# An encoder layer's mixing stage: dilated heads third, latent heads last

## Chip, cores and metric

The kernel runs on one core of a Trainium2 chip. The metric is device time of one execution in microseconds (us), as the median of several. About 0.3% (6.3 us) is what a measurement of this kernel can tell from no change.

## What is computed

A trunk of two layers over 512 tokens of width 1024, in 32-bit floats. Each layer has a gated feed-forward block, a mixing stage with four groups of four heads, a second feed-forward block and a gated per-layer input. Cut to the mixing stage:

```python
z = rms_norm(x, mix_norm[i]) @ w_in[i]
z_na, z_swa, z_dil, z_mla = jnp.split(z, IN_SPLITS, axis=-1)
y_na = na_mixer(z_na, na_bias[i])                 # 8 x 16 neighbourhood, learned bias
y_swa = swa_mixer(z_swa, swa_sink[i], pos)        # band of +-128 tokens, rotary
y_dil = dil_mixer(z_dil, pos)                     # three dilated bands, merged, rotary
y_mla = mla_mixer(z_mla, mla_q_norm[i], mla_w_uq[i], mla_kv_norm[i], mla_w_ukv[i], pos)
y = concatenate([rms_norm(y_na, group_norm[i, 0]), rms_norm(y_swa, group_norm[i, 1]),
                 rms_norm(y_dil, group_norm[i, 2]), rms_norm(y_mla, group_norm[i, 3])])
x = x + y @ w_out[i]
```

`mla_mixer` is the latent one: the projections `cq` (256 wide) and `ckv` (128 wide) are normalised and multiplied by a second pair of weights (`mla_w_uq`, `mla_w_ukv`) to give queries, keys and values; 32 rotary key columns (`kpe`) are shared by its four heads.

## The kernel before

Activations are kept transposed, as tiles of 128 features by 512 tokens. Every 32-bit product is made of three TensorE matmuls on values that are split into a high part and a rest: high by high, high by rest, rest by high (`mm3y`, lines 303 to 305). Weights are loaded as they are (`raw`, by SP's queue), split by ScalarE into `wh` (line 236) and by VectorE, or in the mixing stage mostly by GpSimd, into `wl` (line 237). There are three buffers each of `wh` and `wl`, four of `raw`.

The order on TensorE and on SP is the order in which the program is written (`manual_schedule`). The order on VectorE, ScalarE and GpSimd is laid out when the program is built, by a scheduler. All engines run in order.

In the mixing stage (`mix`) two sequences of work are woven together by hand:

- The **heads** in the order of `heads(l)`: 0 to 3 neighbourhood (`na`), 4 to 7 sliding window (`swa`), 8 to 11 latent (`mla`), 12 to 15 dilated (`dil`). Each passes through six blocks `b`. In blocks 0 to 3 head n's scores are made (`qk`: matmuls of lines 614 to 616 for latent heads, 619 and 620 for the others; row minimum on VectorE, exponential on ScalarE, line 632). In blocks 1 to 4 the head before is transposed (`tr`, line 661, and split into `PT`, lines 664 and 665), in blocks 3 to 5 and block 0 of the next but one its values are multiplied in (`pv`, line 677). `na` and `swa` heads see bands of 256 or 384 keys; `dil` and `mla` heads see all 512.
- The **stream**, a list of generators: projections of eight steps each, then the latent stage's second weights (`d_up`, six steps for two heads), then `part0` to `part3`, the share of the output projection that the first two groups give (eight steps each, `d_part`). A step is the three matmuls of one 128 x 128 weight tile. `STEPS[n] / 6` steps are taken after each block (`pump`). Before head n starts, `need` takes as many steps as it takes until that head's last input is finished, without any attention work in between. Those are not subtracted from the later shares. A value tile is finished (`finish`, transposes of line 590) three steps after its projection; a statistic (`rstat`, line 330) four steps after.

A projection with rotary embedding (`rope`, lines 543 to 552, and `stack`, lines 554 to 574) gives ScalarE four quarter copies (line 547) and two to four half copies. The latent stage does without, but its shared key part is copied into each key tile by a DMA that GpSimd issues (line 814, `big<-kpe`), and its rows are scaled by two statistics (`d_lstat`).

After head 15: `pv(last, 3)`, `pair_end`, then up to seven steps (`TAIL`), the sum of squares of the last group (`rstat`, line 330), up to four steps (`TAIL2`), and `group_end`, which spreads the scale by transposes (line 341), scales and splits the two tiles. Then the output projection of the third group is done for four output tiles (`early`), and that of the last group follows (`out`).

Of the kernel before, what the change touches and what calls it, by code (L numbers as in the profile page):

```python
# [24 lines left out]
EPS = 1e-6  # L25
BIG = 1e30
NT_MIX = 20
STEPS = (11, 11, 11.5, 12.5, 12.5, 11, 9, 9, 8.25, 6.25, 8.25, 8.75, 11.25, 9.25, 9.25, 8.75, 0.5)

PRE, TAIL, TAIL2 = 1, 7, 4  # L30
GAINS = 43

G_FFN1, G_MIX, G_FFN2, G_PLE, G_GRP, G_Q, G_KV = 0, 8, 16, 24, 32, 40, 42
(M_NQ0, M_NK0, M_NV0, M_NQ1, M_NK1, M_NV1, M_SK, M_SQ0, M_SV, M_SQ1, M_CQ0, M_CQ1, M_CKV, M_KPE,
 M_DQ0, M_DK0, M_DV0, M_DQ1, M_DK1, M_DV1, M_END) = range(21)


class Encoder:
# [121 lines left out]
    def plan(self):  # L160
        a = self.a
        full = ((0, 4, 128), (512, 4, 128))
        for l in range(self.depth):
            for w in range(2):
                gu = a["ffn_gu"][l, w]
                for half in range(2):
                    c0, c1 = CUT[half], CUT[half + 1]
                    for f in range(c0, c1, 2):
                        if f == 0:
                            for n, g in enumerate(self.direct(l == w == 0, gu)):  # L170
                                yield g
                                if n == (4 if l == w == 0 else 7):
                                    sums = self.sums(gu[2, 1], gu[3, 1])
                            continue
                        s = self.factors(gu[f, 1], gu[f + 1, 1], sums)
                        d = self.slices((gu[f, 0], full), (gu[f + 1, 0], full))
                        for n, c in enumerate(ORDER):
                            yield s if c == "s" else d
                            if n == 3 and f + 2 < FF:
                                sums = self.sums(gu[f + 2, 1], gu[f + 3, 1])  # L180
                    for m in range(KC):
                        dn = a["ffn_d"][l, w, m]
                        yield from self.each((dn[:, c0:c0 + 8], full), (dn[:, c0 + 8:c1], ((0, c1 - c0 - 8, 128),)))
                if w == 0:
                    for i in range(M_END):
                        if i == M_DQ0:
                            for j in range(2):
                                yield from self.each((a["w_up"][l, j], ((0, 2, 256), (512, 1, 256))))
                        yield from self.each((a["w_in"][l, i], full))
                    for i in range(8):  # L190
                        yield from self.each((a["w_out"][l, i], full))
            for m in range(KC):
                pl = a["ple"][l, m]
                yield from self.each((pl[:, 0:4], ((0, 4, 128),)), (pl[:, 4:10], ((0, 3, 128), (384, 3, 128))))
# [664 lines left out]
    def heads(self, l):  # L859
        nc, a = self.nc, self.a  # L860
# [30 lines left out]

        out = []
        for f, gi, keys in ((na, 0, ("nq{0}", "nk{0}", "nv{0}")), (swa, 1, ("sk", "sq{0}", "sv")),
                            (mla, 2, ("mv{0}",)), (dil, 3, ("dv{0}",))):
            for h in range(4):
                out.append((f, gi, h, [k.format(h // 2) for k in keys]))
        return out

    def mix(self, l, nxt):
        nc, a = self.nc, self.a  # L900
# [16 lines left out]
            ("nv1", self.d_value("nv1", M_NV1, True)),  # L917
            ("sk", self.d_rope("sk", M_SK)), ("sq0", self.d_rope("sq0", M_SQ0, s)),
            ("sv", self.d_value("sv", M_SV)), ("sq1", self.d_rope("sq1", M_SQ1, s)),
            ("cq0", self.d_lat("cq0", 0, M_CQ0)), ("cq1", self.d_lat("cq1", 1, M_CQ1)),  # L920
            ("ckv", self.d_lat("ckv", 2, M_CKV)), ("lstat", self.d_lstat()),
            ("kpe", self.d_kpe()), ("mv0", self.d_up(0)), ("mv1", self.d_up(1)),
            ("dq0", self.d_rope("dq0", M_DQ0, s)),
            ("dk0", self.d_rope("dk0", M_DK0)), ("dv0", self.d_value("dv0", M_DV0)),
            ("dq1", self.d_rope("dq1", M_DQ1, s)), ("dk1", self.d_rope("dk1", M_DK1)),
            ("dv1", self.d_value("dv1", M_DV1)),
        ]
        for _ in self.proj(M_NQ0):
            pass
# [9 lines left out]
        last, prev, pend, rg = None, None, None, None  # L939
# [4 lines left out]
        for n, item in enumerate(todo + [None]):  # L944
            h = None
            if item is not None:
                f, gi, i, keys = item
# [12 lines left out]
            for b in range(6):  # L960
# [231 lines left out]
def _prepare(i):  # L1192
# [28 lines left out]
    ukv = i["mla_w_ukv"][:, :, ukv].reshape(L, 128, 2, 256).transpose(0, 2, 1, 3)  # L1221
    r["w_up"] = np.concatenate([uq, ukv], 3)
    swp = np.concatenate([rng(64), 128 + rng(64), 64 + rng(64), 192 + rng(64)])
    order = np.concatenate([rng(256), 256 + swp, 768 + rng(256), 512 + rng(256)])
    wo = i["w_out"][:, order].reshape(L, KC, 128, KC, 128)
    pm = lambda v, k, m: v.reshape(L, k, 128, -1, m, 128).transpose(0, 3, 2, 4, 1, 5).reshape(L, -1, 128, 8, 128)
    r["w_out"] = np.concatenate([pm(wo[:, 0:4], 4, 2), pm(wo[:, 4:6, :, 0:4], 2, 4), pm(wo[:, 6:8, :, 0:4], 2, 4),
# [38 lines left out]
```

## Time and profile before

| | |
|---|---|
| median of 3 executions | 2105.25 us (2104.72 to 2109.62) |
| the profiled execution's own time | 2106.33 us |
| its span, first to last instruction | 2104.6 us |
| TensorE matmul busy | 2061.2 us, 98% |
| VectorE, ScalarE, GpSimd busy | 65%, 52%, 19% |
| the two mixing stages, first head's scores to the last head's values | 386.7 to 603.9 and 1430.9 to 1645.0 us |

Engines are named PE (TensorE matmul), PEld (its weight loads), DVE (VectorE), ACT (ScalarE), POOL (GpSimd), SP (its queue issues weight loads). A row's line number is that of the kernel before. The duration of a matmul in a row includes its way through the array and overlaps the next one; what a matmul costs in a row of matmuls is the distance from start to start, 0.23 us for 512 columns. PEclk is the granted TensorE clock as a share of 2.4 GHz, so 0.50 is 1.2 GHz.

### The profile page before, as it was taken

How to read it: one execution, taken by the hardware profiler on the slowest of the kernel's cores; microseconds unless marked ns; L12 is line 12 of the kernel's file. 1: busy time of each engine (PE TensorE's matmuls, PEld its weight loads, DVE VectorE, ACT ScalarE, POOL GpSimd, SP SyncE). 2: the span in 40 equal slices, each digit the busy share in tenths (PEclk: the TensorE clock that was granted, in tenths of full speed). 3: DMA queues.
4: the chain of work that ended last, by engine and by line, in shares of the span. 5: the costliest groups of instructions: out<-in, count | busy, mean ns of one | idle time of the engine just before them, and what ended most of it. 6: DMA issues, size and time to landing. Idle time of an engine off the chain costs nothing.

```text
span 2104.6 us, 30073 instructions
## 1 busy us (share of the span) xinstructions
PE 2061.2 (98%) x11028; PEld 1761.4 (84%) x11028; DVE 1365.0 (65%) x2282; ACT 1089.1 (52%) x2057; POOL 393.5 (19%) x391
## 2 busy tenths in 40 slices
PE   8999999999999999999999999999999999999998
PEld 6988988887877988988889889888878789889886
DVE  7654666777777654666766546667787766546655
ACT  6442444687865442444644324437777644334434
POOL 2200101043322200101121002011433321002011
PEclk9999999999999999999999999999999999999999
DMA  7764753323126754753367457433121267457432
GB/s 221 181 163 115 189 135 112 96 66 81 51 61 150 188 145 118 187 140 103 118 148 191 131 137 177 125 102 108 62 81 60 67 167 183 125 144 182 128 93 85
DMA packets 109604, 269.07 MB, mean 128 GB/s; under 512 B 12688, under 2 KB 16912, under 8 KB 109456
## 3 DMA queue, kind: packets, MB, share of 16 engines
q1 hardware_dynamic: 79232, 208.89, 31.3%
q0 software_dynamic: 30080, 58.21, 16.2%
q8 instruction: 86, 1.41, 0.3%
q14 instruction: 62, 0.51, 0.1%
q10 hardware_dynamic: 144, 0.05, 0.0%
HBM read 262.91 MB, written 2.10 MB: 126 GB/s over the span
## 4 chain that ended last, share of the span: by engine, by line
PE 88%; DVE 5%; ACT 3%; DMA 1%; issue 1%; POOL 0%; SPq 0%; DVEq 0%; ACTq 0%; POOLq 0%
PE s L412 16%; PE ps L304 15%; PE ps L303 15%; PE ps L305 15%; PE s L303 6%; PE s L304 6%; PE s L305 6%; PE ps L412 3%; PE pv L677 2%; PE s L661 2%; ACT tmp L547 1%; PE s L619 1%; PE s L620 1%; DVE PT L665 1%; PE s L330 1%
## 5 line engine op out<-in xcount | busy, mean ns | idle before, releaser
L236 ACT ACTIVATE wh<-raw 128x512 fp32r<-128x512 f32 (+2 forms) x668 | 408.2, 612 | 578.9 <-PE ps L304 254.9
L237 DVE TENSOR_TENSOR wl<-raw,wh 128x512 fp32r<-128x512 f32 (+2 forms) x594 | 415.4, 700 | 259.3 <-ACT wh L236 251.6
L256 POOL DMA_DIRECT2D S<-in_ffn_gu x160 | 139.5, 880 | 910.1 <-DMA S<-in_ffn_gu 536.1
L303 PE MATMUL ps<-big,wh 128*128 128x512 f32 x632 | 253.0, 400 | 0.4 <-ACT big L156 0.4
L305 PE MATMUL ps<-big,wl 128*128 128x512 f32 x632 | 247.8, 392 | 3.1 <-DVE wl L237 3.1
L304 PE MATMUL ps<-big,wh 128*128 128x512 f32 x632 | 248.1, 393 | 0.9 <-DVE big L157 0.9
L303 PE MATMUL ps<-act,wh 128*128 128x512 f32 x624 | 248.9, 399 | 0.0
L305 PE MATMUL ps<-act,wl 128*128 128x512 f32 x624 | 244.2, 391 | 3.1 <-DVE wl L237 3.1
L304 PE MATMUL ps<-act,wh 128*128 128x512 f32 x624 | 244.4, 392 | 0.6 <-DVE act L157 0.6
L412 PE MATMUL s<-TC,wh 128*128 128x256 f32 x1280 | 236.1, 282 | 0.7 <-ACT rb L348 0.7
L412 PEld LDWEIGHTS s<-TC,wh 128*128 128x128 f32 x1280 | 205.7, 189 | 10.3 <-ACT rb L348 0.9
L237 DVE TENSOR_TENSOR wl<-S,wh 128x512 fp32r<-128x512 f32 x160 | 110.8, 692 | 122.3 <-ACT wh L236 121.1
L412 PE MATMUL s<-TC,wl 128*128 128x256 f32 x640 | 181.4, 283 | 0.0
L236 ACT ACTIVATE wh<-S 128x512 fp32r<-128x512 f32 x160 | 101.2, 633 | 149.3 <-DMA S<-in_ffn_gu 61.3
L305 PEld LDWEIGHTS ps<-big,wl 128*128 128x128 f32 x632 | 118.9, 188 | 29.9 <-DVE wl L237 4.0
L305 PEld LDWEIGHTS ps<-act,wl 128*128 128x128 f32 x624 | 117.1, 188 | 29.4 <-DVE wl L237 4.0
L304 PEld LDWEIGHTS ps<-big,wh 128*128 128x128 f32 x632 | 119.5, 189 | 21.7 <-DVE big L157 1.9
L303 PEld LDWEIGHTS ps<-big,wh 128*128 128x128 f32 x632 | 119.4, 189 | 20.7 <-ACT big L156 0.8
L237 POOL TENSOR_TENSOR wl<-raw,wh 128x512 fp32r<-128x512 f32 (+1 forms) x74 | 95.9, 1296 | 217.4 <-ACT wh L236 208.6
L304 PEld LDWEIGHTS ps<-act,wh 128*128 128x128 f32 x624 | 117.6, 188 | 20.8 <-DVE act L157 1.3
L303 PEld LDWEIGHTS ps<-act,wh 128*128 128x128 f32 x624 | 117.5, 188 | 19.6
L319 POOL TENSOR_TENSOR acc<-acc,tmp 128x512 f32<-128x512 f32 x48 | 67.1, 1398 | 349.6 <-ACT tmp L318 349.6
(244 smaller groups left out, 4346.7 us busy)
## 6 DMA issues: line engine op xcount, KB each, us to landing
raw<-in_ffn_gu SPq DMA_DIRECT2D x134, 512.0 KB, 5.1
S<-in_ffn_gu POOLq DMA_DIRECT2D x200, 256.0 KB, 4.8
raw<-in_ffn_d SPq DMA_DIRECT2D x64, 512.0 KB, 3.5
S<-in_ffn_gu SPq DMA_DIRECT2D x120, 256.0 KB, 3.8
raw<-in_w_in SPq DMA_DIRECT2D x40, 512.0 KB, 3.6
raw<-in_ffn_gu SPq DMA_DIRECT2D x44, 256.0 KB, 3.8
raw<-in_ffn_d SPq DMA_DIRECT2D x32, 256.0 KB, 2.6
raw<-in_w_out SPq DMA_DIRECT2D x16, 512.0 KB, 3.5
```

The costliest lines, as they stand in the source:

```text
L236: self.hold(nc.scalar.activation(hi, r, AF.Copy))
L237: self.hold(self.side().tensor_tensor(out=lo, in0=r, in1=hi.bitcast(F32), op=ALU.subtract))
L256: nc.gpsimd.dma_start(t, src, accum_op=ALU.add)
L303: nc.tensor.matmul(ps, lhsT=wh[:, k], rhs=x[:, 0], start=start and k == 0, stop=False)
L304: nc.tensor.matmul(ps, lhsT=wh[:, k], rhs=x[:, 1], start=False, stop=False)
L305: nc.tensor.matmul(ps, lhsT=wl[:, k], rhs=x[:, 0], start=False, stop=stop and k == last)
L319: self.hold(eng.tensor_tensor(out=acc, in0=acc, in1=sq, op=ALU.add))
L330: nc.tensor.matmul(ss[:, t:t + 1], lhsT=p[:, t * 128:(t + 1) * 128], rhs=self.ones, start=i == t == 0, stop=i == len(parts) - 1 and t == 3 ...
L412: nc.tensor.matmul(ps, lhsT=v[:, k], rhs=x[:, e], start=start and k == i == 0, stop=k == 3 and i == 2, skip_group_check=True)
L547: nc.scalar.activation(sw[32 * b:32 * b + 32], p[32 * o:32 * o + 32], AF.Copy)
L661: nc.tensor.transpose(tp[:, t * 128:(t + 1) * 128], h["P"][t][:, o:o + 128], self.ident)
L677: nc.tensor.matmul(pv[:, c], lhsT=vb, rhs=h["pt"][b][:, i, c], start=b == 0 and i == 0, stop=b == 3 and i == 1, skip_group_check=True)
```

## The change

The dilated heads become heads 8 to 11 and the latent heads 12 to 15. The stream's projections, the weights' load order, the group norm weights, the rows of the output projection and the four `STEPS` shares of either group move with them; no share is changed in size, and no instruction is added or dropped on TensorE. The changed kernel's lines are one or two lower.

```diff
-STEPS = (11, 11, 11.5, 12.5, 12.5, 11, 9, 9, 8.25, 6.25, 8.25, 8.75, 11.25, 9.25, 9.25, 8.75, 0.5)
+STEPS = (11, 11, 11.5, 12.5, 12.5, 11, 9, 9, 11.25, 9.25, 9.25, 8.75, 8.25, 6.25, 8.25, 8.75, 0.5)
...
                     for i in range(M_END):
-                        if i == M_DQ0:
-                            for j in range(2):
-                                yield from self.each((a["w_up"][l, j], ((0, 2, 256), (512, 1, 256))))
                         yield from self.each((a["w_in"][l, i], full))
+                    for j in range(2):
+                        yield from self.each((a["w_up"][l, j], ((0, 2, 256), (512, 1, 256))))
...
         for f, gi, keys in ((na, 0, ("nq{0}", "nk{0}", "nv{0}")), (swa, 1, ("sk", "sq{0}", "sv")),
-                            (mla, 2, ("mv{0}",)), (dil, 3, ("dv{0}",))):
+                            (dil, 2, ("dv{0}",)), (mla, 3, ("mv{0}",))):
...
-            ("cq0", self.d_lat("cq0", 0, M_CQ0)), ("cq1", self.d_lat("cq1", 1, M_CQ1)),
-            ("ckv", self.d_lat("ckv", 2, M_CKV)), ("lstat", self.d_lstat()),
-            ("kpe", self.d_kpe()), ("mv0", self.d_up(0)), ("mv1", self.d_up(1)),
             ("dq0", self.d_rope("dq0", M_DQ0, s)),
             ("dk0", self.d_rope("dk0", M_DK0)), ("dv0", self.d_value("dv0", M_DV0)),
             ("dq1", self.d_rope("dq1", M_DQ1, s)), ("dk1", self.d_rope("dk1", M_DK1)),
             ("dv1", self.d_value("dv1", M_DV1)),
+            ("cq0", self.d_lat("cq0", 0, M_CQ0)), ("cq1", self.d_lat("cq1", 1, M_CQ1)),
+            ("ckv", self.d_lat("ckv", 2, M_CKV)), ("lstat", self.d_lstat()),
+            ("kpe", self.d_kpe()), ("mv0", self.d_up(0)), ("mv1", self.d_up(1)),
...
-        gc = (0, 1, 3, 2)[gi]
```

Three places show what moves; all are in layer 0, and layer 1 reads the same. First **TensorE at the end of the mixing stage**, from the sum of squares of the last group (its input is `acc`) to the transposes that spread the scale (`rc`). Before:

```order
L330 MATMUL s_6090<-ones,acc_6050 128x1 x4
L303 MATMUL ps_6080<-keep_4549,wh_6063 128x512
L304 MATMUL ps_6080<-keep_4549,wh_6063 128x512
L305 MATMUL ps_6080<-keep_4549,wl_6064 128x512
L303 MATMUL ps_6080<-keep_5170,wh_6063 128x512
L304 MATMUL ps_6080<-keep_5170,wh_6063 128x512
L305 MATMUL ps_6080<-keep_5170,wl_6064 128x512
L303 MATMUL ps_6080<-keep_5174,wh_6063 128x512
L304 MATMUL ps_6080<-keep_5174,wh_6063 128x512
L305 MATMUL ps_6080<-keep_5174,wl_6064 128x512
L341 MATMUL s_6108<-ident,rc_6095 128x128 x4
```

The same place in the changed kernel, from the last two steps of `part3`:

```order
L304 MATMUL ps_6064<-keep_5106,wl_5992 128x512
L302 MATMUL ps_6064<-keep_5110,wh_5991 128x512
L303 MATMUL ps_6064<-keep_5110,wh_5991 128x512
L304 MATMUL ps_6064<-keep_5110,wl_5992 128x512
L329 MATMUL s_6100<-ones,acc_6085 128x1 x4
L340 MATMUL s_6108<-ident,rc_6105 128x128 x4
```

The three steps between the sum and the transposes are gone; ahead of the sum, between `pair_end` and it, three steps stand where seven stood.

Next **GpSimd around the first copies of the shared key part** (`big<-kpe`; `wl` is a weight's rest), ahead of head 8 in the kernel before:

```order
L786 TENSOR_TENSOR raw_4759<-raw_4759,rg_4750 128x512
L237 TENSOR_TENSOR wl_4835<-raw_4832,wh_4834 128x512
L237 TENSOR_TENSOR wl_4861<-raw_4832,wh_4860 128x256
L814 DMA big_4844<-kpe_4788 64x1024
L237 TENSOR_TENSOR wl_4927<-raw_4924,wh_4926 128x512
L814 DMA big_4850<-kpe_4788 64x1024
```

and ahead of head 12 in the changed one:

```order
L784 TENSOR_TENSOR raw_5404<-raw_5404,rg_5395 128x512
L236 TENSOR_TENSOR wl_5447<-raw_5444,wh_5446 128x512
L236 TENSOR_TENSOR wl_5473<-raw_5444,wh_5472 128x256
L236 TENSOR_TENSOR wl_5541<-raw_5538,wh_5540 128x512
L812 DMA big_5456<-kpe_5410 64x1024
L812 DMA big_5462<-kpe_5410 64x1024
```

One more weight's rest stands ahead of the first copy.

Last **VectorE at the same place**, from the first instruction that reads the `kpe` projection (`ps`) to the split of the finished key part (`kpe`). Before, `P` and `PT` are rows of the attention of heads 6 and 7:

```order
L771 TENSOR_TENSOR tmp_4654<-ps_4660,tmp_4654 64x512
L772 TENSOR_TENSOR tmp_4655<-ps_4660,tmp_4655 64x512
L626 ISA P_4768,ne_4695<-s_4765,swa_mask,nsink 128x256
L626 ISA ne_4695 128x1
L665 TENSOR_TENSOR PT_4785<-s_4781,PT_4785 128x384
L773 TENSOR_TENSOR tmp_4654<-tmp_4654,tmp_4655 64x512
L640 TENSOR_TENSOR l_4554<-l_4554,se_4771 128x4
L665 TENSOR_TENSOR PT_4807<-s_4804,PT_4807 128x256
L643 RECIPROCAL rl_4774<-l_4554 128x8
L802 TENSOR_TENSOR tmp_4813<-ps_4798,raw_4759 128x512
L154 TENSOR_TENSOR kpe_4788<-tmp_4654,kpe_4788 64x512
```

In the changed kernel:

```order
L769 TENSOR_TENSOR tmp_5342<-ps_5348,tmp_5342 64x512
L770 TENSOR_TENSOR tmp_5343<-ps_5348,tmp_5343 64x512
L800 TENSOR_TENSOR tmp_5427<-ps_5420,raw_5404 128x512
L771 TENSOR_TENSOR tmp_5342<-tmp_5342,tmp_5343 64x512
L800 TENSOR_TENSOR tmp_5439<-ps_5432,raw_5404 128x512
L157 SCALAR_TENSOR_TENSOR big_5429<-tmp_5427,big_5429 128x512
L809 TENSOR_TENSOR tmp_5454<-ps_5450,P_5402 64x512
L154 TENSOR_TENSOR kpe_5410<-tmp_5342,kpe_5410 64x512
```

No attention row is left among them, and the latents' own work (scaling of the first two queries, lines 800, and of a key, line 809) has moved ahead of the key part's split.

## Rows read from the trace of the kernel before

**Rows 1.** The page: busy time by engine, and the chain that ended last

```profile
PE 2061.2 (98%) x11028; PEld 1761.4 (84%) x11028; DVE 1365.0 (65%) x2282; ACT 1089.1 (52%) x2057; POOL 393.5 (19%) x391
PE 88%; DVE 5%; ACT 3%; DMA 1%; issue 1%; POOL 0%; SPq 0%; DVEq 0%; ACTq 0%; POOLq 0%
```

**Rows 2.** PE's timeline ahead of head 8: start, duration, [idle before, releaser]

```profile
485.75 0.39 PE L305 MATMUL ps<-keep,wl 128*128 128x512 f32 x1
488.13 0.66 PE L590 MATMUL s<-ident,tmp 128*128 128x128 f32 x4 [1.99 <-DVE tmp L585]
...
489.62 0.77 PE L614 MATMUL s<-big,big 128*128 128x512 f32 x1 [0.60 <-DMA big<-kpe]
...
1530.96 0.66 PE L590 MATMUL s<-ident,tmp 128*128 128x128 f32 x4 [1.99 <-DVE tmp L585]
```

**Rows 3.** Stretches: length, PE PEld DVE ACT POOL busy (instructions), PEclk, DMA

```profile
488.94:495.75 6.81, 6.21 (x17) 4.80 (x17) 4.21 (x8) 3.91 (x8) 1.39 (x1) 0.50 0.17 37
1530.96:1545.00 14.04, 13.12 (x68) 10.22 (x69) 11.38 (x20) 9.84 (x22) 5.45 (x5) 1.00 0.50 128
```

**Rows 4.** DVE ahead of head 8: its timeline, two groups of that stretch

```profile
477.97 0.70 DVE L771 TENSOR_TENSOR tmp<-ps,tmp 64x512 f32<-64x512 f32 x1 [1.27 <-PE ps L305]
...
487.38 0.69 DVE L585 TENSOR_TENSOR tmp<-ps,P 128x512 f32<-128x512 f32 x1
...
L665 DVE TENSOR_TENSOR PT<-s,PT 128x384 fp32r<-128x384 f32 (+1 forms) x2 | 1.0, 486 | 0.0
...
L626 DVE CUSTOM_DVE_ANT_0 P<-s,swa_mask,nsink 128x256 f32<-128x256 f32 x1 | 0.5, 486 | 0.0
```

**Rows 5.** POOL's timeline ahead of head 8, the chain's DMA, the copies' landing times

```profile
483.56 0.59 POOL L814 DMA_DIRECT2D big<-kpe  x1
484.31 1.30 POOL L237 TENSOR_TENSOR wl<-raw,wh 128x512 fp32r<-128x512 f32 x1
...
483.56 5.92 DMA big<-kpe
...
DMA to landing us min/median/max: 3.3/4.6/5.9
```

**Rows 6.** PE's timeline at the end of layer 0's mixing stage

```profile
604.23 0.47 PE L303 MATMUL ps<-keep,wh 128*128 128x512 f32 x1
...
609.12 0.95 PE L330 MATMUL s<-ones,acc 128*128 128x1 f32 x8
609.93 0.49 PE L303 MATMUL ps<-keep,wh 128*128 128x512 f32 x1
...
612.11 0.60 PE L341 MATMUL s<-ident,rc 128*128 128x128 f32 x4
```

**Rows 7.** DVE's and POOL's timelines at the same place

```profile
606.90 1.36 DVE L319 TENSOR_TENSOR acc<-acc,tmp 128x512 f32<-128x512 f32 x1
...
610.41 1.01 POOL L334 TENSOR_TENSOR rc<-rc,nhalf 128x4 f32<-128x4 f32 x1
```

**Rows 8.** PE's waits from 496 to 603 us: total, times, longest

```profile
PE pv L677 <- DVE PT L665: 1.0, 3, 0.5
PE s L661 <- ACT P L632: 0.7, 1, 0.7
```

**Rows 9.** Stretches of heads 5 and 10, columns as in rows 3

```profile
448.09:460.57 12.48, 12.48 (x74) 10.89 (x73) 10.00 (x23) 9.15 (x23) 4.12 (x4) 1.00 0.01 2
517.33:531.66 14.33, 13.09 (x65) 9.83 (x64) 12.86 (x19) 12.74 (x25) 3.44 (x3) 1.00 0.10 38
```

**Rows 10.** ACT's quarter copies, 380 to 650 us: xcount | busy, mean ns

```profile
L547 ACT ACTIVATE tmp<-ps 32x512 f32<-32x512 f32 x28 | 16.5, 590 | 0.4
```

**Rows 11.** Two more long waits of PE, and the stretch behind the second

```profile
643.34 0.50 PE L305 MATMUL ps<-act,wl 128*128 128x512 f32 x1 [2.25 <-DVE wl L237]
...
1068.92 0.88 PE L341 MATMUL s<-ident,rc 128*128 128x128 f32 x4 [2.15 <-POOL rc L334]
...
1069.20:1072.60 3.40, 3.40 (x12) 2.72 (x11) 1.38 (x2) 1.23 (x2) 0.00 (x0) 0.50 0.09 15
```

More of the change, by code (lines that the diff above doesn't have):

```diff
@@ L33 @@
 G_FFN1, G_MIX, G_FFN2, G_PLE, G_GRP, G_Q, G_KV = 0, 8, 16, 24, 32, 40, 42
-(M_NQ0, M_NK0, M_NV0, M_NQ1, M_NK1, M_NV1, M_SK, M_SQ0, M_SV, M_SQ1, M_CQ0, M_CQ1, M_CKV, M_KPE,
- M_DQ0, M_DK0, M_DV0, M_DQ1, M_DK1, M_DV1, M_END) = range(21)
+(M_NQ0, M_NK0, M_NV0, M_NQ1, M_NK1, M_NV1, M_SK, M_SQ0, M_SV, M_SQ1, M_DQ0, M_DK0, M_DV0, M_DQ1, M_DK1, M_DV1,
+ M_CQ0, M_CQ1, M_CKV, M_KPE, M_END) = range(21)
 class Encoder:
@@ L707, in group_end @@
         rg = self.rspread(rc, "rg")
-        gc = (0, 1, 3, 2)[gi]
         for j, y in enumerate(self.ys):
             t = self.big() if gi == 3 else self.keep()
-            nc.vector.scalar_tensor_tensor(y, y, self.g(l, G_GRP, 2 * gc + j), rg,
+            nc.vector.scalar_tensor_tensor(y, y, self.g(l, G_GRP, 2 * gi + j), rg,
                                            op0=ALU.mult, op1=ALU.mult)
@@ L1223, in _prepare @@
     swp = np.concatenate([rng(64), 128 + rng(64), 64 + rng(64), 192 + rng(64)])
-    order = np.concatenate([rng(256), 256 + swp, 768 + rng(256), 512 + rng(256)])
+    order = np.concatenate([rng(256), 256 + swp, 512 + rng(512)])
     wo = i["w_out"][:, order].reshape(L, KC, 128, KC, 128)
```

## The prediction

> **What bounds the kernel.** The page comes first: TensorE is busy for 98% of the span and carries 88% of the chain that ended last [rows 1]. No matmul is added or dropped, so the time moves only where TensorE stands still, or where it runs at 1.2 instead of 2.4 GHz. I then read PE's timeline for gaps in the mixing stages. Two places matter, the same in both layers. Ahead of head 8, five steps are forced through without attention, and the chain of the latents' first keys and values ends late: the value transposes wait for VectorE, then the first score waits for a copy of the shared key part [rows 2]. In layer 0 the stretch behind that wait shows a granted clock of 0.50; in layer 1 the same wait is followed by 1.00 [rows 3]. And at the stage's end ten steps lie under the last group's norm [rows 6]. What is small: waits of 1.0 and 0.7 us on `PT` and `P` in heads 8 to 16 [rows 8].
>
> **What moves: the steps.** Up to head 8, 1 + 3 steps are taken ahead (`PRE`, and three to finish `nv0`), 2 are forced before head 2, and `STEPS` gives 87.5: 93 of the stream. In the kernel before, `mv0` is finished after 98, so 5 are forced. Changed, head 8 needs only `dv0`, long done. Up to head 12 the shares give 126, in all 132. `mv0` now ends with 56 (first two groups) + 48 (dilated) + 33 (latents, statistics, `kpe`) + 6 + 3 = 146, so 14 steps are forced: five of `kpe`, six of `d_up`, three behind. The stream has 181 steps in both. The kernel before has used 4 + 2 + 5 + 2 + 158 = 171 when the last head ends and keeps ten; the changed one 4 + 2 + 14 + 158 = 178 and keeps three.
>
> **Term 1, the wait ahead of head 8 goes.** A matmul starts at 485.75 and costs 0.23; the transposes start at 488.13, so 2.15 us are lost. The two `pv` matmuls of 256 columns behind the transposes cost 0.12 each from 488.54, and the score starts at 489.62: 0.84 more. Layer 1's wait of 1.99 is as long [rows 2]. 3.0 us a layer: -6.0. Next late there is nothing: dil0's inputs were finished in head 7. With it goes layer 0's slow stretch, 6.21 us busy at half the clock [rows 3]: -3.1.
>
> **Term 2, a wait ahead of head 12 comes.** The chain is the same as before, so I move its rows. Before, VectorE starts on `kpe` at 477.97 and has scaled the first values at 487.38 + 0.69 = 488.07: 10.1 us, of which 1.5 are attention [rows 4] that the changed order has already behind it: 8.6. TensorE now has nine steps there (0.70 each by 604.23 to 609.12 for seven [rows 6]), 6.3 us. So the transposes wait 2.3; they and `pv` take 0.9, and TensorE stands at the first score 9.5 us after `kpe`, with 7.1 of work done: at least 2.4 lost. The score also needs the copy. Its issue came 5.6 us after `kpe` (483.56); now one more weight's rest of 1.3 stands ahead of it on GpSimd's queue, 6.9, and that weight's high part needs a `wh` buffer that the forced steps free only after the value's matmuls. Landing takes 3.3, 4.6 or 5.9 (least, median, most) [rows 5]: at 10.2, 11.5 or 12.8, which loses 3.1, 4.4 or 5.7. I take the median, 4.4, since a 512 KB load is issued beside it as before; the bounds are 2.4 and 5.7. Two layers: +8.8. Queued behind the waiting score are head 12's first steps; nobody else is held up.
>
> On the copy a rule speaks against this. The Trainium skill ("DMA: Bandwidth & Descriptors", section "Anatomy of one DMA — SWDGE (gpsimd) path") gives such a DMA 2.0 us and its bytes at 436 GB/s, by my estimate 2.6 us for 256 KB. By it the copy would land with the value's chain, the wait would be 2.4 and the whole sum 4.0 lower. The trace does not agree: none of its eight copies landed in under 3.3 us.
>
> **Term 3, the stage's end loses its cover.** Before, seven steps run from 604.23 to 609.12, then the sum of squares; its input is ready at 606.90 + 1.36 = 608.26 [rows 6, 7]. With three steps TensorE is there at 606.3 and waits 2.0. From the sum's start to the end of GpSimd's power it was 609.12 to 611.42, 2.3 us, and nothing is left to do under it: the transposes start at 608.3 + 2.3 = 610.6 instead of 612.11. Seven steps of work (4.8) have left this stretch, and it is only 1.5 shorter: +3.3 a layer, +6.6. Bounds: the add at 606.90 took 1.36 and would take half of it with GpSimd idle (2.6); the changed order puts a weight's split on ScalarE ahead of the square and its rest on VectorE ahead of the add (3.9). Behind the transposes all stays: `early` covers scaling and splitting as before.
>
> **Term 4, the rotary projections move** from heads 9 to 13 to heads 4 to 8, and the latents' the other way. Each gives ScalarE four quarter copies of 0.59 [rows 10] and two (query) or four (key) half copies, at about the same price: 3.6 or 4.8 us. Head 5 has ScalarE at 9.15 of 12.48 us [rows 9]; two splits and two squares leave (about 2.5), a query and a key come (8.4): some 15 in 12.5, a backlog that heads 6 and 7 take in. Such crowding exists before, too: head 10 has 12.74 of 14.33 and TensorE loses 1.24 there [rows 9]. The waits that go with the old places are 1.7 as shown, four of them, each about 0.2 longer by starts as at 488.13: 2.5 a layer [rows 8]. I take the same at the new ones, net 0. Bounds: -2.5 (none waits), +2.5 (each of four loses 1.24).
>
> **Term 5, the clock.** Five waits of TensorE of about 2 us stand in the trace: one ahead of head 8 in each layer [rows 2], one like 643.34 in each layer, and 1068.92 [rows 11]. Two were followed by 0.50 [rows 3, 11], at 3.1 and half of 3.40 = 1.7 us: 2.4 each. The changed kernel has four such places, two a layer. At 2 in 5: 4 x 0.4 x 2.4 = +3.8; bounds 0 and +9.6.
>
> The rest is free: the loads' order on SP follows the stream's, each issued well ahead; group norm weights and output rows only change place.
>
> **Sum:** -6.0 - 3.1 + 8.8 + 6.6 + 0 + 3.8 = +10.1 on the profiled execution's 2106.3: 2116.4. That execution lies 1.1 above the median of the runs shown, so I predict 2115.3.
>
> **Rivals.**
> The copy and the value's chain end together (wait 2.4 ahead of head 12), the end costs its lower bound 2.6, and no clock falls: -0.6 + 2.6 = 2.0 a layer, +4.0 - 3.1 = +0.9: 2106.1, no change. For it: nine steps without attention let VectorE catch up. Against: one more GpSimd rest ahead of the copy. By the landing times, of which only the shortest come near, I give it 0.18. The rule of the Trainium skill on such DMAs ("DMA: Bandwidth & Descriptors", the section above) is on its side.
>
> Not slower: VectorE is relieved. Rotary work beside wide heads is what makes `PT` late; beside band heads, whose rows are half as wide, it makes nothing late, and latent heads beside `part` steps have slack. Then the four waits go (-2.5), the wait ahead of head 12 is at 2.4 and the end at 2.6: -0.5 a layer, -1.0 - 3.1 = -4.1: 2101.1. It decides from where heads 4 to 8 lose less than some 0.5 us a layer. For it: VectorE is at 12.86 of 14.33 in head 10, 10.00 of 12.48 in head 5 [rows 9]. Against: ScalarE's 15 in 12.5. 0.20, a third of it under the bound for faster.
>
> Much slower: ScalarE's backlog under heads 5 to 8 holds up weights' high parts and `PT`; +2.5 a layer on the forecast: 2120.3. 0.17.
>
> **Chances.** Forecast 0.45. Slower by over 0.3% (6.3 us, about what a measurement of this kernel tells from no change) is the forecast and the last rival: 0.62; within 0.3%: 0.18 + 0.14 = 0.32; faster: 0.06. The range goes from the first rival's 2106 to 2123, the last one's with one more slow stretch; it leaves out the second rival's 0.20 at most.
>
> **What would show it.** In PE's timeline: no wait over 1 us ahead of head 8; ahead of head 12 a wait of the transposes for VectorE of about 2 us and one of the first score for `big<-kpe` of about 2; at the end about 2 us before the sum of squares and 1.3 before the transposes. I am wrong if the end costs under 2 us a layer, or if heads 4 to 8 show waits of over 4 us together.

## The result, and the profile after

The changed kernel takes 2130.05 us (median of 4 executions, 2127.57 to 2130.63) against 2106.16 for the kernel before (4 executions, 2104.72 to 2109.62): a ratio of 1.0114, 95% interval 1.0101 to 1.0127. It is slower, by 24 us where 10 were forecast, and above the range's end of 2123. The profiled execution took 2130.63 us with a span of 2128.9, 24.3 longer than the span before.

The page of the changed kernel, where [rows 1] stood: its span, the engines' busy time, and the chain that ended last. The same matmuls are 2073.4 us busy in place of 2061.2, and TensorE's share of the chain fell from 88% to 86%.

```profile
span 2128.9 us, 30071 instructions
PE 2073.4 (97%) x11028; PEld 1768.3 (83%) x11028; DVE 1364.2 (64%) x2282; ACT 1089.4 (51%) x2057; POOL 391.8 (18%) x391
PE 86%; DVE 6%; ACT 3%; issue 3%; DMA 1%; POOL 1%; SPq 0%; DVEq 0%; ACTq 0%; POOLq 0%
```

**Where it went.** For both traces I took the time from each matmul's start to the next one's, less the median of that distance for its line and shape, and summed it by head (a head runs from its first score to the next head's). What lies in a stretch of granted clock 0.50 and is not idle time is called slow. Layer 0 / layer 1, in us:

| stretch | before | after | of it slow, before | slow, after |
|---|---|---|---|---|
| heads 1 to 4 | 3.8 / 2.5 | 5.1 / 2.4 | 0 | 0 |
| heads 5 to 7 | 3.9 / 3.8 | 7.6 / 7.6 | 0.2 / 0 | 1.6 / 1.7 |
| heads 8 to 10 | 5.9 / 4.2 | 2.4 / 2.4 | 2.9 / 0 | 0 |
| head 11, forced steps, head 12 | 0.5 / 0.5 | 6.0 / 6.1 | 0 | 1.6 / 1.7 |
| heads 13 to 15 | 1.1 / 1.1 | 0.6 / 0.6 | 0 | 0 |
| the 68 us behind head 15, with the stage's end | 8.9 / 8.9 | 15.1 / 15.9 | 0 | 2.7 / 4.7 |
| from there to the next mixing stage or the kernel's end | 6.8 / 2.6 | 4.1 / 2.5 | 1.6 / 0 | 0 / 0.4 |

The differences add up to 24.0, the 24.3 of the spans. The losses lie in three places: heads 5 to 7, the forced steps ahead of head 12, and the end. Heads 8 to 10 give 5.3 back. Of layer 1's 4.7 at the end, 1.9 lie further on, at 1709 us, behind a wait for a weight that the kernel before has too, at full clock behind it.

**Heads 5 and 6.** PE's timeline in layer 0; there were no such waits here before.

```profile
458.76 0.45 PE L676 MATMUL pv<-PT,big 128*128 128x384 f32 x1 [1.07 <-DVE PT L664]
...
471.78 0.39 PE L676 MATMUL pv<-PT,big 128*128 128x256 f32 x1 [1.46 <-DVE PT L664]
...
473.95 0.44 PE L676 MATMUL pv<-PT,big 128*128 128x384 f32 x1 [0.58 <-DVE PT L664]
```

The two heads' stretches, columns as in [rows 3]; the first answers to the first of [rows 9]. ScalarE is busy for 12.74 us in head 5 (9.15 before) and VectorE for 12.68 of 13.80 in head 6; TensorE's own work in them is 12.3 and 11.1 us long (length less loss before).

```profile
449.25:464.63 15.38, 14.31 (x74) 12.20 (x73) 10.00 (x22) 12.74 (x29) 6.25 (x6) 0.89 0.16 51
464.63:478.43 13.80, 11.51 (x63) 9.11 (x62) 12.68 (x24) 11.15 (x25) 3.80 (x3) 1.00 0.11 39
```

VectorE's timeline around the two longest waits of head 6, and GpSimd's operation beside it: the rests of the first group's normed tiles (`keep<-y,keep`) stand between the rows of `PT`, and the second one takes 1.78 us where the first takes 0.68.

```profile
470.71 0.68 DVE L154 TENSOR_TENSOR keep<-y,keep 128x512 fp32r<-128x512 f32 x1
471.32 0.41 DVE L664 TENSOR_TENSOR PT<-s,PT 128x256 fp32r<-128x256 f32 x1
471.65 1.78 DVE L154 TENSOR_TENSOR keep<-y,keep 128x512 fp32r<-128x512 f32 x1
473.36 0.54 DVE L664 TENSOR_TENSOR PT<-s,PT 128x384 fp32r<-128x384 f32 x1
...
470.98 1.90 POOL L236 TENSOR_TENSOR wl<-raw,wh 128x512 fp32r<-128x512 f32 x1 [3.02 <-ACT wh L235]
```

**Ahead of head 12.** PE's timeline, where [rows 2] stood ahead of head 8. The wait is not the score's: TensorE stands ahead of a step of the forced run, since the `ps` buffer that the step writes (there are three) is read by VectorE's scaling of a key, line 809. The first score, at 557.46, waits for nothing.

```profile
551.75 0.40 PE L304 MATMUL ps<-keep,wl 128*128 128x512 f32 x1
554.46 0.47 PE L302 MATMUL ps<-keep,wh 128*128 128x512 f32 x1 [2.32 <-DVE tmp L809]
...
555.69 1.12 PE L589 MATMUL s<-ident,tmp 128*128 128x128 f32 x4 [0.31 <-DVE tmp L584]
...
557.46 0.63 PE L613 MATMUL s<-big,big 128*128 128x512 f32 x1
```

VectorE and GpSimd there, each from its own timeline, and the landing times of the eight copies ([rows 4, 5] before).

```profile
551.85 1.74 DVE L154 TENSOR_TENSOR kpe<-tmp,kpe 64x512 fp32r<-64x512 f32 x1
553.62 0.69 DVE L809 TENSOR_TENSOR tmp<-ps,P 64x512 f32<-64x512 f32 x1
...
551.78 1.27 POOL L236 TENSOR_TENSOR wl<-raw,wh 128x512 fp32r<-128x512 f32 x1 [1.10 <-ACT wh L235]
553.89 1.14 POOL L812 DMA_DIRECT2D big<-kpe  x2 [0.84 <-DVE kpe L154]
...
DMA to landing us min/median/max: 2.9/3.6/4.9
```

**The end.** PE's timeline, as in [rows 6].

```profile
617.38 0.39 PE L304 MATMUL ps<-keep,wl 128*128 128x512 f32 x1
619.85 1.55 PE L329 MATMUL s<-ones,acc 128*128 128x1 f32 x8 [2.08 <-DVE acc L318]
622.74 1.11 PE L340 MATMUL s<-ident,rc 128*128 128x128 f32 x4 [1.34 <-POOL rc L333]
```

**The clock.** Stretches of 0.50 in the changed kernel, apart from the kernel's last ones (columns as in [rows 3]): behind head 5's wait, behind the forced steps, at the end, and one further on. Layer 1 has the first three again, at 1511.03, 1606.61 and 1671.46: 30.7 us in all. Before there were two [rows 3, 11].

```profile
459.73:463.14 3.41, 3.41 (x10) 2.85 (x9) 1.65 (x3) 3.34 (x7) 1.94 (x2) 0.50 0.26 101
555.30:558.71 3.41, 3.10 (x10) 2.57 (x10) 2.51 (x5) 1.01 (x2) 0.00 (x0) 0.50 0.68 133
620.16:626.99 6.83, 5.49 (x19) 4.71 (x19) 2.60 (x5) 1.86 (x3) 1.01 (x1) 0.50 0.00 0
...
1709.01:1712.42 3.41, 3.30 (x8) 2.09 (x8) 3.41 (x8) 1.69 (x3) 0.87 (x1) 0.50 0.79 235
```

The timed executions also have their span and mean granted clock; (1 - clock) x span is the clock that it lost, in us at full speed. The clock is recorded to three decimals, so one such value is good to about 1 us, and some 5 us of it lie in the kernel's last stretch, which every kernel has. It is 17.0 to 21.3 in the four executions of the changed kernel, mean 19.2, and 4.2 to 14.8, mean 8.7, in the 53 of the kernel before for which it is on record. So about 10 of the 24 us go with the clock in the timed executions too; the slow columns of the table above, from the profiled ones, differ by 9.7.

### The profile page after: what moved, and what is told of

Its sections match the earlier page's. It is cut to its first block, busy times and chain, and to the rows that moved or that the text cites. A ratio compares the mean times of both kernels' runs of the same rounds, so it can differ in the third digit from the quotient of the medians.

```text
span 2128.9 us, 30071 instructions
## 1 busy us (share of the span) xinstructions
PE 2073.4 (97%) x11028; PEld 1768.3 (83%) x11028; DVE 1364.2 (64%) x2282; ACT 1089.4 (51%) x2057; POOL 391.8 (18%) x391
## 3 DMA queue, kind: packets, MB, share of 16 engines
q8 instruction: 86, 1.41, 0.3%
## 4 chain that ended last, share of the span: by engine, by line
PE 86%; DVE 6%; ACT 3%; issue 3%; DMA 1%; POOL 1%; SPq 0%; DVEq 0%; ACTq 0%; POOLq 0%
PE s L411 16%; PE ps L303 14%; PE ps L302 14%; PE ps L304 14%; PE s L302 6%; PE s L303 6%; PE s L304 6%; PE ps L411 3%; PE pv L676 2%; PE s L660 1%; ACT tmp L546 1%; DVE PT L664 1%; PE s L329 1%; ACT wh L235 1%; PE s L618 0%
```

## The experiments

Twelve kernels. The time is the median; the ratio is to executions of the kernel before on the same chip; the lost clock is the mean over the kernel's executions. The kernels were timed on several chips, on which the median of the kernel before was 2104.3 to 2106.7 us, and the changed kernel was timed only once, with the first result. A difference in us from the changed kernel is therefore uncertain by some 2 us, and the ratios are the safer comparison.

| kernel | us | ratio, 95% interval | lost clock |
|---|---|---|---|
| changed | 2130.05 | 1.0114 (1.0101 to 1.0127) | 19.2 |
| e_tail | 2120.53 | 1.0078 (1.0056 to 1.0099) | 11.1 |
| e_noforce14 | 2115.36 | 1.0054 (1.0036 to 1.0073) | 11.6 |
| e_both | 2113.36 | 1.0040 (1.0027 to 1.0052) | 7.8 |
| e_warm | 2121.65 | 1.0082 (1.0066 to 1.0098) | 8.5 |
| e_side | 2124.80 | 1.0090 (1.0073 to 1.0107) | 14.9 |
| e_swap | 2123.88 | 1.0088 (1.0073 to 1.0103) | 20.2 |
| b_notail | 2116.95 | 1.0061 (1.0046 to 1.0076) | 13.2 |
| b_noforce | 2107.92 | 1.0020 (1.0011 to 1.0029) | 7.6 |
| e_q6 | 2123.53 | 1.0086 (1.0072 to 1.0100) | 13.8 |
| e_nof_warm | 2112.92 | 1.0039 (1.0025 to 1.0053) | 7.4 |
| b_warm | 2101.77 | 0.9987 (0.9978 to 0.9996) | 6.1 |
| b_best | 2106.74 | 1.0002 (0.9993 to 1.0011) | 5.6 |

### The end's cover: e_tail, b_notail

e_tail is the changed kernel with

```diff
-(..., 8.25, 6.25, 8.25, 8.75, 0.5)
+(..., 6.5, 4.5, 6.5, 7, 0.5)
```

> The changed kernel with seven steps fewer under heads 12 to 15, so that ten are left for the stage's end, as in the kernel before. Theory (the end lost its cover, and the clock fell behind its waits): the end's loss by starts of matmuls, 15.1 and 15.9 us in the two layers of the changed kernel, returns to the 8.9 of the kernel before, the stretches of 0.50 at the end go: -13, about 2117 us. If only the waits belong to the cover, and not the clock: -6 to -7, about 2123. Rival (heads 12 to 15 are bound by ScalarE or VectorE and don't get shorter): about 2130.

Measured: 2120.5, 9.5 less than the changed kernel (7.6 by the ratios). Its end loses 8.8 and 8.9 us, the numbers of the kernel before; the sum of squares and the transposes wait for nothing, and the clock is 1.00. PE's timeline and the stretch:

```profile
616.64 0.95 PE L329 MATMUL s<-ones,acc 128*128 128x1 f32 x8
619.63 0.60 PE L340 MATMUL s<-ident,rc 128*128 128x128 f32 x4
...
613.00:626.00 13.00, 13.00 (x64) 10.85 (x63) 8.08 (x12) 5.22 (x9) 3.53 (x3) 1.00 0.19 48
```

The end was right, the rest of the expectation was not: heads 12 to 15, with seven steps fewer, lose 4.2 us a layer where they lost 2.4. That is 3.6 of the 13 given back.

b_notail is the other side: the kernel before, its order kept.

```diff
-(..., 11.25, 9.25, 9.25, 8.75, 0.5)
+(..., 13.25, 11.25, 12, 11.5, 0.5)
```

> The kernel before with its own order, but more steps under heads 12 to 15, so that three are left for the stage's end in place of ten. Theory (the loss at the end is a matter of cover and not of the order): the end loses 12 to 16 us a layer in place of 8.9, with one or two stretches of 0.50 behind it: 2111 to 2118 us. Rival (what the fuller heads 12 to 15 gain makes up for it, or the end's waits come from the latent heads being last): 2105 to 2108.

Measured: 2116.95. Its end loses 14.4 and 15.7, in layer 0 with the waits of the changed kernel to the hundredth and as long a slow stretch. So the cost of the end belongs to the steps that are left for it and not to the heads that come last.

```profile
612.58 1.83 PE L330 MATMUL s<-ones,acc 128*128 128x1 f32 x8 [2.08 <-DVE acc L319]
615.75 1.11 PE L341 MATMUL s<-ident,rc 128*128 128x128 f32 x4 [1.34 <-POOL rc L334]
...
612.45:619.28 6.83, 5.36 (x19) 4.73 (x20) 1.87 (x4) 1.52 (x3) 1.01 (x1) 0.50 0.00 0
```

### The clock: e_warm, e_nof_warm

e_warm is the changed kernel with

```diff
-        self.pump(TAIL)
+        self.pump(TAIL); self.warm(16)
         rg = self.rstat(self.gacc, 256)
...
-        self.pump(TAIL2)
+        self.pump(TAIL2); self.warm(10)
+    def warm(self, n):
+        bc = self.small()
+        for i in range(n):
+            self.nc.tensor.transpose(bc[:, i % 4 * 128:i % 4 * 128 + 128], self.ident, self.ident)
```

> The changed kernel with 16 transposes of the identity ahead of the sum of squares at the stage's end and 10 ahead of the transposes of its root, results unused: TensorE is busy where it waited. Theory (the clock at the end falls because TensorE stood still there): no stretch of 0.50 behind the end, the 2.7 and 4.7 us that ran slow there return, the waits stay: -7, about 2123 us. Rival (the clock falls for another reason, or the transposes don't hold it): no gain, 2130, or up to 2 us slower where the transposes outlast the waits.

Measured: 2121.65, 8.4 less (6.7 by the ratios), with work added. The data that TensorE waits for come no earlier, yet the clock stays at 1.00 at both ends (this is layer 0's; layer 1's row reads 1.00 too):

```profile
612.85 1.91 PE L1097 MATMUL s<-ident 128*128 128x128 f32 x16
615.09 1.02 PE L329 MATMUL s<-ones,acc 128*128 128x1 f32 x8 [0.33 <-DVE acc L318]
615.97 1.29 PE L1097 MATMUL s<-ident 128*128 128x128 f32 x10
617.45 0.65 PE L340 MATMUL s<-ident,rc 128*128 128x128 f32 x4 [0.19 <-POOL rc L333]
...
612.00:626.00 14.00, 13.48 (x79) 11.43 (x78) 7.46 (x12) 4.47 (x8) 1.01 (x1) 1.00 0.14 39
```

With e_nof_warm below, none of four ends with transposes has a slow stretch, against 11 of 12 with the same three steps and no transposes. So the standing still causes the slow stretch, and at the end that costs (2.7 us a layer) about as much as the waits themselves (2.9 more than before). From head 15's first score to the next stage's first matmul that reads a `TC` tile (line 411), TensorE takes 79.9 and 80.8 us in the two layers, where the changed kernel takes 82.2 and 83.0: the transposes gain 4.4 us there. The rest of the 8.4 is not theirs. In this execution no slow stretch came behind head 5 in either layer, nor behind the forced steps in layer 0, and those places have no transposes.

e_nof_warm is e_noforce14 (below) with `warm(5)` and `warm(11)` at the same places.

> The kernel with 14 steps more under heads 8 to 11, and 5 transposes of the identity ahead of the sum of squares at the end and 11 ahead of the transposes of its root. Theory (waits and clock add up as separate costs): the slow stretches behind the end, 3.4 and 1.8 us there, go: 2110 us, still slower than the kernel before by what the end lacks in cover (2 a layer) and by heads 5 to 7. Rival (the clock falls elsewhere instead, since heads 5 and 11 wait for 1.3 and 2.2 us too): 2113 to 2116.

Measured: 2112.9, at the lower end of the rival's range, lost clock 7.4 after 11.6. Both ends are free of slow stretches. In layer 0 one came behind the wait of head 5 and one behind that of head 11, where the profiled execution of e_noforce14 has none. The intervals of the two kernels' ratios overlap, so a gain over e_noforce14 is likely but not shown.

### The forced steps: e_noforce14, e_both, b_noforce

e_noforce14 is the changed kernel with

```diff
-(..., 11.25, 9.25, 9.25, 8.75, 8.25, 6.25, 8.25, 8.75, 0.5)
+(..., 14.85, 12.85, 12.85, 12.35, 7.85, 6.25, 8.25, 8.75, 0.5)
```

> The changed kernel with 14 steps more under heads 8 to 11, so that the latents' first values are finished without forced steps ahead of head 12; the end keeps three steps. Theory (the forced chain makes the wait): the 5.5 us that head 11, the forced steps and head 12 lose more than before (1.6 of it clock) fall to 1 at most: -9, about 2121 us. Rival (dilated heads are too full): PT and the scores wait for VectorE or ScalarE in heads 8 to 11, by 2 us a layer or more, and the time is 2125 to 2130.

Measured: 2115.4, better than expected, and for another reason. No step is forced, but the wait is still there, inside head 11 and for the same kind of VectorE work, now behind rows of attention. Heads 11 and 12 lose 4.5 and 4.8 (1.6 of the latter slow) in place of 6. What vanished is the loss of heads 8 and 9, 2.3 us a layer, now 0.3: ScalarE is nearly as full in head 8 (11.79 of 13.00 us below; 12.71 of 13.75 in the changed kernel), but TensorE has 3.6 steps more to do meanwhile. The rest of the gain is slow clock: in this execution none came behind head 5 or, in layer 0, behind head 11, and less of it at the end. PE's timeline in head 11, and most of head 8:

```profile
547.58 0.50 PE L302 MATMUL ps<-keep,wh 128*128 128x512 f32 x1 [2.05 <-DVE tmp L800]
...
489.00:502.00 13.00, 13.00 (x71) 11.04 (x70) 8.36 (x18) 11.79 (x26) 5.62 (x5) 1.00 0.19 66
```

e_both has both edits (heads 8 to 11 as here; 6.1, 4.5, 6.5 and 7 for heads 12 to 15).

> Both edits of the shares of steps together: 14 steps more under heads 8 to 11, seven fewer under heads 12 to 15, ten left for the end. Theory (the two costs are independent): -13 - 9 = -22, about 2108 us, the kernel before within 0.3%; what is left is heads 5 to 9, which lose 5 to 6 us a layer more than before, against the forced wait ahead of head 8 that is gone. Rival (they are not independent: shorter latent heads or fuller dilated ones lose elsewhere): 2114 or more.

Measured: 2113.4, just under the rival's 2114. Its mechanism holds: with few steps beside them, heads 12 and 13 lose 2.9 and 4.5 us where e_noforce14 loses 2.3 and 1.0.

b_noforce is the kernel before without forced steps ahead of head 8:

```diff
-(11, 11, 11.5, 12.5, 12.5, 11, 9, 9, 8.25, 6.25, 8.25, 8.75, 11.25, 9.25, 9.25, 8.75, 0.5)
+(11, 11, 11.5, 12.5, 12.5, 11.5, 11, 12, 7.25, 6.25, 8.25, 8.75, 10.5, 9.25, 8.5, 8, 0.5)
```

> The kernel before with 5.5 steps more under heads 5 to 7 and fewer under heads 8 and 12 to 15, so that no step is forced ahead of head 8; the end keeps its cover. Theory (the forced chain makes the wait ahead of head 8, worth 3 us a layer and some clock): 2097 to 2099 us. Rival (the chain's steps only move the same lateness of VectorE and of the copy into heads 7 and 8): 2103 to 2106.

Measured: 2107.9, 0.2% slower than the kernel before (0.1 to 0.3%) and worse than the rival says. The wait moves into head 7, for VectorE's scaling of a latent query, and heads 8 to 10 lose 6.7 us a layer:

```profile
485.00 0.50 PE L303 MATMUL ps<-keep,wh 128*128 128x512 f32 x1 [1.79 <-DVE tmp L802]
...
496.51 0.50 PE L614 MATMUL s<-big,big 128*128 128x512 f32 x1 [0.61 <-ACT P L632]
```

In either order, then, the latents' short products (0.7 to 1.4 us each, three `ps` buffers) reach VectorE faster than it clears them. In both orders spreading the forced steps moved that wait and did not remove it.

### Heads 5 to 7: e_swap, e_side, e_q6

e_swap gives ScalarE less to do for a rotary projection. It leaves out the exchange of halves, so its rotary queries and keys, and its result, are other numbers; it only serves to see what the copies cost:

```diff
-        for b in range(4):
-            o = b ^ 1
-            nc.scalar.activation(sw[32 * b:32 * b + 32], p[32 * o:32 * o + 32], AF.Copy)
+        nc.scalar.activation(sw, p, AF.Copy)
```

> The changed kernel with the four quarter copies of a rotary projection replaced by one copy of the whole tile: the halves are not exchanged, so the rotary queries and keys are other ones, and ScalarE does 0.6 us for each of them in place of 2.4. Theory (ScalarE's backlog under the rotary work): heads 5 to 8, that lose 1.5, 2.3, 1.15 and 1.7 us without slow clock, lose under 2 us together: 5 us a layer gained, about 2120, or 2117 without the slow stretch behind head 5. Rival (VectorE, held up by GpSimd, is what makes PT late): heads 5 and 6 stay within 1 us of what they lose, only head 8 (ScalarE busy for 12.7 of 13.75 us) gains, 2126.

Measured: 2123.9. Heads 5 and 7 lose 0.2 each in place of 1.5 (without slow clock) and 1.15, head 8 1.0 in place of 1.7: there it was ScalarE. Head 6 got worse, 3.5 and 3.9 without slow clock, where e_warm and e_noforce14, that run head 5 at full clock as this kernel does, lose 2.3: there it is not ScalarE. VectorE's timeline has no idle time (over 0.15 us) from 459.65 to 468.98 us, around that wait. Each theory holds in some heads. The two stretches and head 6's wait:

```profile
445.93:458.41 12.48, 12.48 (x75) 10.91 (x73) 10.48 (x23) 9.14 (x24) 6.21 (x6) 1.00 0.24 83
458.41:475.23 16.82, 13.78 (x64) 11.23 (x62) 10.94 (x23) 11.15 (x25) 3.77 (x3) 0.80 0.09 32
...
467.45 0.58 PE L674 MATMUL pv<-PT,big 128*128 128x256 f32 x1 [2.49 <-DVE PT L662]
```

e_side takes GpSimd's arithmetic away in heads 5 and 6:

```diff
-            if n == 3:
+            if n in (3, 7):
                 self.mixing = True
+            if n == 5:
+                self.mixing = False
```

> The changed kernel with GpSimd's arithmetic (the rotary sine product and the weights' rests) given to VectorE during heads 5 and 6. Without slow clock these two heads lose 1.5 and 2.3 us a layer. Theory (VectorE's additions and subtractions from SBUF, 0.7 us alone and 1.75 beside a GpSimd operation, hold PT up): the long ones are gone, the two heads lose 1 us or less together, 3 us a layer gained, 2124 us or, with the slow stretch behind head 5 gone, 2121. Rival (VectorE or ScalarE simply has too much to do there; VectorE gets some five operations of 0.7 more): the two heads lose 5 us or more, 2132 to 2136.

Measured: 2124.8, heads 5 and 6 lose 1.3 and 3.2: 4.5 together, against 3.8 without slow clock. The theory is refuted, and the rival's 5 us are not reached either. Without GpSimd beside it VectorE's operations are short again (the two rests of the normed tiles take 1.28 together, where the second alone took 1.78), but there are more of them, and head 6 still waits, first for a mask row and then for `PT`:

```profile
467.74 0.39 PE L618 MATMUL s<-big,big 128*128 128x256 f32 x1 [1.15 <-DVE ne L625]
...
470.28 0.45 PE L676 MATMUL pv<-PT,big 128*128 128x384 f32 x1 [0.60 <-DVE PT L664]
...
468.48 1.28 DVE L154 TENSOR_TENSOR keep<-y,keep 128x512 fp32r<-128x512 f32 x2
```

e_q6 takes two operations out of VectorE's queue in head 6:

```diff
-            self.split(t, y)
+            self.split(t, y, eng=nc.gpsimd if gi == 0 else None)
```

> The changed kernel with the rests (low parts) of the first group's two normed tiles formed by GpSimd in place of VectorE: two operations of 0.7 to 1.8 us leave VectorE's queue in head 6. Theory (in head 6 the rotary key and the first group's end stand in VectorE's queue ahead of PT): head 6 loses 1.3 us or less without slow clock, where it was 2.3, 1 us a layer, 2128 us or, with less slow clock behind head 5, 2124. Rival (another operation is the late one, or GpSimd's longer work beside VectorE stretches others as much): head 6 loses 2 us or more, 2130.

Measured: 2123.5; head 6 loses 1.33 and 1.35, about as expected. Its waits are down to these:

```profile
467.44 0.39 PE L676 MATMUL pv<-PT,big 128*128 128x256 f32 x1 [0.36 <-DVE PT L664]
...
471.82 0.44 PE L676 MATMUL pv<-PT,big 128*128 128x384 f32 x1 [0.35 <-DVE PT L664]
```

That gives 2 us for both layers. The rest of the 6.5 (5.9 by the ratios) goes with the lost clock (13.8 after 19.2): in this execution no slow stretch came behind head 5, which the edit does not touch.

### Transposes in the old wait: b_warm, b_best

b_warm leaves the old order alone and keeps TensorE busy in the wait that the change was to remove:

```diff
             p = self.small()
+            for b in range(16 if key == "mv0" else 0):
+                nc.tensor.transpose(p[:, b % 4 * 128:b % 4 * 128 + 128], self.ident, self.ident)
...
+                    if n == 8 and b == 0:
+                        self.warm(5)
                     self.qk(h, b)
```

> The kernel before with 16 transposes of the identity ahead of the value transposes and 5 ahead of the first score of head 8: TensorE is busy in the wait that the change took away. Theory (the slow stretches behind head 8 come from that wait): none there any more, -2 us in the mean, 2102 to 2103; the wait itself stays. Rival (the transposes outlast the wait, or the clock falls behind the stage's end instead): 2104 to 2107.

Measured: 2101.8, ratio 0.9987 (0.9978 to 0.9996); lost clock 6.1 in the mean of 11 executions, and 8.8 in the 15 of the kernel before on the same chip. The interval lies below 1, but 0.13% is less than the 0.3% that counts as a change here: it is the fastest kernel of the study by very little. The transposes fill the 1.99 of [rows 2], and the clock behind it is 1.00 in both layers, here layer 0's. In this execution 0.50 came at 1067.94, as in the kernel before, and also at 641.28 and 1682.34, at waits like that of 643.34 in [rows 11], which were followed by 1.00 there:

```profile
486.23 1.91 PE L590 MATMUL s<-ident 128*128 128x128 f32 x16
488.37 0.66 PE L592 MATMUL s<-ident,tmp 128*128 128x128 f32 x4 [0.23 <-DVE tmp L585]
...
485.00:492.00 7.00, 6.76 (x44) 5.54 (x43) 6.54 (x11) 3.44 (x7) 1.37 (x2) 1.00 0.60 150
```

b_best adds e_q6's edit for the second group (`gi == 1`), whose end falls into head 10 of the old order.

> The kernel before with 16 and 5 transposes of the identity in its wait ahead of head 8, and the rests of the second group's two normed tiles formed by GpSimd in place of VectorE (1.29 us of VectorE in head 10, where a rotary query and the group's end meet, as they do in head 6 of the changed order). Theory (the same crowding of VectorE's queue): head 10 loses 1.3 us or less in place of 2.07, -1.5 us on the kernel with the transposes alone: 2100.3. Rival (in head 10 ScalarE, busy for 12.74 of 14.33 us, is late by itself): head 10 stays at 2.0, 2102.

Measured: 2106.7, no gain on the kernel before (2106.7 on the same chip): head 10 loses 4.4 us where it lost 2.1, waiting for ScalarE's exponentials. These come late because VectorE's row minima do. Below PE's two waits stand VectorE's operation ahead of the minima and GpSimd's two rests beside it, and last the same VectorE operation in the kernel before.

```profile
519.79 0.66 PE L663 MATMUL s<-ident,P 128*128 128x128 f32 x4 [0.73 <-ACT P L634]
523.48 0.49 PE L616 MATMUL s<-big,big 128*128 128x512 f32 x1 [1.63 <-ACT P L634]
...
518.99 3.02 DVE L570 SCALAR_TENSOR_TENSOR big<-tmp,big 64x512 fp32r<-64x512 f32 x2
518.49 2.97 POOL L154 TENSOR_TENSOR keep<-y,keep 128x512 fp32r<-128x512 f32 x2 [2.60 <-ACT keep L153]
...
521.29 1.41 DVE L570 SCALAR_TENSOR_TENSOR big<-tmp,big 64x512 fp32r<-64x512 f32 x2
```

VectorE's two operations take 3.02 us beside GpSimd's work in place of 1.41. That is 1.6 more, as long as the longer wait. So what was taken from VectorE came back as a longer operation, the rival that e_q6 named. This is read from the trace, and no run tests it by itself.

## Why the prediction was wrong in size

The direction was right, and TensorE waits ahead of head 12 and at the end, as forecast. Two steps failed: term 4, put at 0, and term 5, the chance and the number of slow stretches. The sum by its terms, both layers, the measured waits without slow clock from the table above:

| term | forecast | measured |
|---|---|---|
| 1, the wait ahead of head 8 and its slow stretch go | -9.1 | about -9 |
| 2, the wait ahead of head 12 | +8.8 | +7.7 |
| 3, the end's cover | +6.6 | +5.8 |
| 4, rotary projections in heads 4 to 8 | 0 | about +8 |
| 5, the clock | +3.8 | +12.7 |
| the rest | 0 | -1 |

Terms 1 and 4 share heads 5 to 10, where the loss rises by 2.2, and the traces do not part them. With the forecast's -9.1 for what went, 11.3 came, 3.2 of it slow; the 8 of term 4 rests on that.

**Term 1** holds: no step is forced ahead of head 8, head 7 loses 1.15 where it lost 3.57, and no slow stretch follows.

**Term 2** had nearly the right price, in part by luck, and half the mechanism. VectorE's chain was right: 8.6 us forecast from `kpe` to the scaled values, 8.9 measured (546.76, its first row on `kpe`, to 555.64, the end of line 584). TensorE waits for it in a place that I had not looked at, the reuse of a `ps` buffer, since nine steps in a row need more than three of them. The copy was wrong. It was issued 7.1 us behind `kpe` (6.9 forecast) but landed in 2.9 and not in the median 4.6 of [rows 5], before the score needed it. The rule of the Trainium skill that I set aside ("DMA: Bandwidth & Descriptors", section "Anatomy of one DMA — SWDGE (gpsimd) path"; 2.6 us by my estimate) comes nearer to this copy than the row I chose. The eight here took 2.9 to 4.9, so neither gives them all. What makes up the price is the 0.85 to 1.05 that head 12 itself loses more, which the forecast did not have.

By my estimate 1.1 us of the 2.3 lies in one operation: VectorE's rest of `kpe` took 1.74 beside a GpSimd operation that began first, at 551.78, and 0.69 in the kernel before, where none had begun ahead of it. The same operation of VectorE on `keep` took 1.78 in head 6, beside one of GpSimd from 470.98 to 472.88, while the `PT` row between them, which reads PSUM, was not stretched (0.41). The Trainium skill ("SBUF — State Buffer", section "SBUF: two separate sides") has it that a VectorE operation with two SBUF inputs and a GpSimd operation that reads SBUF exclude each other for a whole instruction; the rows agree. e_side shows what that is worth in heads 5 and 6: nothing, since GpSimd's work has to be done by VectorE then.

**Term 3** was right, waits (2.08 and 1.34 for "about 2" and "1.3") and price; e_tail and b_notail show it from both sides.

**Term 4** failed. The step was to take the waits of the old places for the new ones. I added up ScalarE for head 5 (15 us in 12.5), called it a backlog that heads 6 and 7 take in, and bounded it by one head of before, head 10. But a head's rows of `PT` are needed within the head: a backlog of ScalarE is a wait at once. The 15 us were not reached either: ScalarE is busy for 12.74 us in head 5, since the key's four half copies (2.5 us) come only in head 6, and that was still over TensorE's 12.3. And I did not add up VectorE for head 6, where the first group's end already stood; with a rotary key beside it VectorE is busy for 12.68 us where TensorE has 11.1 of work. The rival that ScalarE holds heads 5 to 8 up named this, and priced it with the same bound, +2.5 a layer where the waits came to about 4. e_swap shows ScalarE's part (heads 5 and 7, some of 8) and e_q6 VectorE's (head 6).

**Term 5** failed by more. The chance of 2 in 5 came from five waits. With three steps left for it, the end had a slow stretch in 11 of 12 cases (the changed kernel, e_side, e_swap, e_q6, e_noforce14 and b_notail, two layers each), the forced steps ahead of head 12 in 10 of 12 (with e_tail and e_warm in place of the last two). The wait of 1.07 in head 5 had one in 6 of 14, and I had not counted it, as it stood in no row of before. The price of 2.4 came out near by its mean only, 2.0: it is 1.6 to 1.7 us behind heads 5 and 11, and 2.7 at the end, where two waits follow each other and the stretch is twice as long. The six such places give 12.0; the 1.9 at 1709 and 0.4 in the kernel's last stretch, less the 1.6 that is gone behind 1068.92, make the 12.7.

**What I named as refuting** came to pass in one half: heads 4 to 8 show waits of over 4 us together (5.0 in layer 0). The end cost more than 2 us a layer.

What stays open: why heads 1 to 4 lose 1.2 us more in layer 0 (head 3 does so in one layer or the other in several kernels, both orders), and how the clock chooses among equal waits.

## What to carry to other kernels

When work moves into another stretch, add up every engine for each head that receives it, with what already stands in its queue, against TensorE's work there: where the sum is larger, TensorE waits, even if the next stretch has room. The difference was less than the loss here: 0.4 us in head 5 and 1.6 in head 6, which lost 1.5 and 2.3 at full clock. Price each wait of TensorE with the slow clock behind it: here that was nearly half of the whole loss, and transposes of a constant in the end's waits gave back 4.4 us without moving any work. Keep work in hand for the end of a stage, whichever part comes last.

## What was not expected of the hardware

Behind the wait of 1.07 us in head 5 the granted clock was 0.50 for 3.41 us in 6 of 14 cases and 1.00 in the others, in the same instructions. Executions of one kernel differ in their lost clock too: the kernel before ran 2099.97 us with 4.2 lost, and 2109.47 with 14.8 on another chip. Where transposes of a constant filled the waits, in e_warm, e_nof_warm and b_warm, the clock behind them was 1.00 in both layers. And taking an operation from VectorE to GpSimd can cost VectorE as much as it saves: in b_best two operations of VectorE took 3.02 us in place of 1.41 beside the work that GpSimd had been given.
